# Per-token sums of squares of the differential heads: from columns beside a loaded square to rows at four column positions, and back by way of HBM

## The chip, the cores and the metric

The kernel is one program on one core of a Trainium2 chip. The metric is the device time of one execution in microseconds (us). The chip's engines run side by side and wait for each other by semaphores: TensorE (PE) multiplies matrices (a weight load, LDWEIGHTS, puts the stationary operand into the array, then a MATMUL streams the moving operand past it), VectorE (DVE) and ScalarE (ACT) work on tiles of up to 128 partitions, GpSimd (POOL) does small work and issues some of the transfers (DMAs), and SyncE (SP) issues most transfers. Each engine runs its own instructions in order.

## The reference, cut to what matters

One layer of a decoder: a modulated RMS norm, a joint input projection, two attention branches, gates, an output projection, a gated MLP with a causal convolution, and a last norm. D_MODEL is 1024, SEQ is 512, and all data are float32. The change touches one place, the RMS norm of each differential head's output:

```python
def _diff_attention(q, k, v, lam, lam_init, subln_g, slopes):
    ...
        p = jax.nn.softmax(scores, axis=-1)
        a = p[:, :, 0] - lam * p[:, :, 1]
        return jnp.einsum('bhqs,bshe->bqhe', a.astype(v.dtype), v)
    ...
    out = _rmsnorm(out, subln_g) * (1.0 - lam_init)
```

There are four heads. For each of the 512 tokens of a head, the mean of 128 squares is needed, its inverse root, and a multiplication of the 128 values by that root.

## The kernel before, in words

The program is laid out by hand as a list of matmuls that PE runs in a written order; the other engines' instructions are put in order by a scheduler with priorities. Between about 130 and 235 us PE works on the four differential heads. For each head it makes scores (`sd`), transposes the softmaxed blocks (`td`), multiplies by the values (`od`, a tile with 128 channels as partitions and 512 tokens in a row), and between these it is given other work in steps of three matmuls: projections `pq` and `pk`, gates `pga` and `pgd`, branch products `pA`. Each such step is a tick of `fill`; `after(n, fn)` runs `fn` n ticks later. The tables `STAT_LAG`, `ROW_LAG` and `NORM_LAG` hold, for each head, in how many ticks three things follow the head's `od`.

First, `stats`, STAT_LAG ticks after `od`. ACT has squared `od` into `sq`. Four matmuls with a 128x128 block of `sq` as stationary and one column of ones as moving give `pss`, 128 tokens on partitions and four blocks in columns. DVE takes `pss` over into `ms` (mean of squares plus an epsilon that is scaled by the softmax sums; `rstd_start`). POOL raises it to the power -0.5 and makes one Newton step in four small instructions; the last one writes four columns of the tile `cols`.

Second, `to_rows`, ROW_LAG ticks after `stats`. PE transposes a 128-column window of `cols` (the PE row is called `rs`), ACT copies 32 rows of the result (`rs0p` to `rs3p`), POOL writes four rows to HBM (`rs0d` to `rs3d`) and reads them back broadcast over 128 partitions (`rb`).

Third, `spread`, NORM_LAG ticks after `stats`. DVE multiplies the head's output `of` by `rb`, and ACT and DVE split it into a high and a low part (`vvh`, `vvl`), which the products `pB` use from 237.56 us on.

The tiles `od`, `pss` and `rs` share one PSUM bank (tag "v", one buffer): each must be read out before PE may write the next. The tiles `rs0p` to `rs3p` share one small SBUF buffer (tag "part").

Of the kernel before, what the change touches and what calls it, by code (L numbers as in the profile page):

```python
# [8 lines left out]
F32 = mybir.dt.float32  # L9
F32R = mybir.dt.float32r  # L10
AF = mybir.ActivationFunctionType
ALU = mybir.AluOpType
PSUM = bass.MemoryType.PSUM

P = 128
# [3 lines left out]
NT = S // P  # L19
# [8 lines left out]
HP = 100000  # L28
# [3 lines left out]
G1_AT = 12  # L32
M5_AT = 4
STAT_LAG = (6, 6, 6, 6)
ROW_LAG = (8, 8, 6, 7)
NORM_LAG = (34, 34, 34, 24)
VA_AT = 5
SWA_FILL = (2, 1, 6, 2, 2, 2, 2, 5, 0)
DIFF_FILL = (3, 2, 4, 2)
NCOL = 161  # L40
# [7 lines left out]
def kernel(  # L48
# [19 lines left out]
    nc = tc.nc  # L68
# [3 lines left out]
    def pool(name, bufs=1, space=None, stack=ctx):  # L72
        kw = {} if space is None else {"space": space}
        return stack.enter_context(tc.tile_pool(name=name, bufs=bufs, reuse_waits="tile", **kw))

    cpool = pool("const")
# [3 lines left out]
    dp = pool("rows", space=bass.MemoryType.DRAM)  # L80

    def bank(tag, bufs, shape, name, dt=F32):
        return ps.tile(shape, dt, tag=tag, bufs=bufs, name=name)
# [10 lines left out]
    def vbank(name, shape=(P, S)):  # L94
        return bank("v", 1, list(shape), name)
# [4 lines left out]
    def to_rows(dst, lo, n, name):  # L100
        turned = vbank(name, (P, P))
        nc.tensor.transpose(turned, cols[:, lo + n - P : lo + n], ident)
        part = cpool.tile([32, P], F32, tag="part", name=name + "p")
        with tc.high_priority(offset=2 * HP):
            nc.scalar.copy(part, turned[96:])
        d = dp.tile([n, P], F32, name=name + "d")
        nc.gpsimd.dma_start(d, part[32 - n :])
        nc.gpsimd.dma_start(dst, d.rearrange("k q -> (k q)").partition_broadcast(P))
# [10 lines left out]
    def split(hi, lo, src):  # L119
        return nc.scalar.copy(hi, src), nc.vector.tensor_sub(lo, src, hi.bitcast(F32))  # L120

    def mm3(o, lh, ll, rh, rl, start, stop):
        nc.tensor.matmul(o, lh, rh, start=start, stop=False)  # L123
        nc.tensor.matmul(o, lh, rl, start=False, stop=False)  # L124
        nc.tensor.matmul(o, ll, rh, start=False, stop=stop)  # L125
# [4 lines left out]
    ones = cpool.tile([P, P], F32, name="ones")  # L130
# [5 lines left out]
    mhalf = cpool.tile([P, 4], F32, name="mhalf")  # L136
# [3 lines left out]
    cols = cpool.tile([P, NCOL + 64], F32, name="cols")  # L140
# [8 lines left out]
    root_in = [None]  # L149

    def rstd_start(ssq, n, d, wpool, plus=None):
        ms = wpool.tile([P, n], F32, tag="rs_a", bufs=3, name="ms")
        if plus is None:
            nc.vector.tensor_scalar(ms, ssq, 1.0 / d, EPS, ALU.mult, ALU.add)
        else:
            root_in[0] = nc.vector.scalar_tensor_tensor(ms, ssq, 1.0 / d, plus, ALU.mult, ALU.add)
        r0 = wpool.tile([P, n], F32, tag="rs_c", bufs=3, name="r0")
        nc.gpsimd.tensor_tensor(r0, ms, mhalf[:, :n], ALU.pow)
        return ms, r0
# [92 lines left out]
    ddf = cpool.tile([P, 512], F32, name="ddf")  # L252
    nc.gpsimd.iota(ddf, [[1, 512]], base=-384, channel_multiplier=-1, allow_small_or_imprecise_dtypes=True)
    nc.gpsimd.affine_select(ddf, ddf, [[-1, 512]], ALU.is_ge, NEG, base=384, channel_multiplier=1)
    eps = cpool.tile([P, 1], F32, name="eps")
    nc.gpsimd.memset(eps, EPS)

# [57 lines left out]
    for p in range(KT // 2):  # L315
        for hf in range(2) if p >= 2 else (None,):
            sl = ALL if hf is None else HALVES[hf]
            sq, xx = (a.rearrange("p (a s) -> p a s", a=2)[:, :, sl] for a in (sqs[p], xT[:, p]))
# [15 lines left out]
    r0 = pp.tile([P, NT], F32, tag="rs_c", bufs=3, name="r0")  # L334
    nc.scalar.activation(r0, stat[:, :, 0], AF.Sqrt, bias=eps, scale=1.0 / D)
    ms = pp.tile([P, NT], F32, tag="rs_a", bufs=3, name="ms")
# [59 lines left out]
    for k in range(KT):  # L396
        n = k + 1
# [24 lines left out]
    ap = pool("att", stack=at)  # L422
# [129 lines left out]
    def after(n, fn):  # L552
        later.append([n, fn])
# [175 lines left out]
    emptied, summed = {}, {}  # L729

    def diff_values(h):
        aTh, aTl = aTs[h]
        o = vbank(f"od{h}")
        for k in range(NT):
            q0 = k * P
            mm3(
                o[:, q0:], vv[0][:, h, k * P : (k + 1) * P], vv[1][:, h, k * P : (k + 1) * P],
                aTh[:, k * AW + q0 : k * AW + 512], aTl[:, k * AW + q0 : k * AW + 512],
                k == 0, k == NT - 1,
            )  # L740
        sq = big.tile([P, S], F32, tag="sq2", name=f"sq{h}")
        of = big.tile([P, S], F32, tag=("kvA", "kvB")[h % 2], name=f"of{h}")
        with tc.high_priority(offset=HP):
            nc.scalar.activation(sq, o, AF.Square)
            emptied[h] = nc.scalar.activation(of, o, AF.Copy, scale=sublnc)

        def stats():
            pss = vbank(f"pss{h}", (P, NT))
            for n in range(NT):
                nc.tensor.matmul(pss[:, n : n + 1], sq[:, n * P : (n + 1) * P], ones[:, 0:1], start=True, stop=True)  # L750
            rs = cols[:, NCOL + NT * h : NCOL + NT * h + NT]
            l0, e0 = sums[h][:, 0], sums[h][:, 1]
            nc.gpsimd.tensor_tensor(e0, l0, l0, ALU.mult)
            nc.gpsimd.tensor_scalar_mul(e0, e0, EPS)
            with tc.high_priority(offset=HP):
                ms, r0 = rstd_start(pss, NT, P, ap, plus=e0)
                summed[h] = root_in[0]
                t = ap.tile([P, NT], F32, tag="rs_b", bufs=3, name="rt")
                nc.gpsimd.tensor_tensor(t, r0, r0, ALU.mult)
                nc.gpsimd.tensor_tensor(t, t, ms, ALU.mult)  # L760
                nc.gpsimd.tensor_scalar_add(t, t, -3.0)
                nc.gpsimd.tensor_tensor(rs, t, r0, ALU.mult)
            last = h == DIFF_HEADS - 1
            rb = big.tile([P, S], F32, tag="sq2", name="rb3") if last else ap.tile([P, S], F32, tag="rb", name=f"rb{h}")

            def spread():
                with ExitStack() as place:
                    for b in recent:
                        place.enter_context(tc.issue_after(b.ins))
                    if not last:  # L770
                        place.enter_context(tc.issue_after(summed[h + 1].ins))
                    nc.vector.tensor_mul(of, of, rb)
                with tc.high_priority(offset=HP), ExitStack() as place:
                    if not last:
                        place.enter_context(tc.issue_after(emptied[h + 1].ins))
                    split(vv[0][:, h], vv[1][:, h], of)

            after(ROW_LAG[h], lambda: to_rows(rb, NCOL + NT * h, NT, f"rs{h}"))
            after(NORM_LAG[h], spread)

        after(STAT_LAG[h], stats)


# [114 lines left out]
    for s in range(4 * DIFF_HEADS):  # L898
        h, n = divmod(s, NT)
# [983 lines left out]
```

## Time and profile before

| what | value |
|---|---|
| median of three runs | 676.37 us (676.16 to 676.6) |
| profiled execution, its own time | 676.23 us |
| span of its instructions | 674.4 us |
| PE busy | 664.4 us, 99% of the span |
| DVE, ACT, POOL busy | 564.3, 400.7, 84.9 us |
| granted PE clock, mean | 0.997 |

The profiled execution lies 1.83 us over its span and 0.14 us under the median. In the rows that are shown later, a timeline row reads: start in us, length in us, engine, line of the kernel, operation, output<-inputs, shape, and how many were merged into the row; in brackets stands how long the engine was idle before, and what ended that. A MATMUL's shape names the array's rows and columns in use (128*128) and what streams past. A float32 matmul shows as two records, since it is made in two passes.

### The profile page before, as it was taken

The numbers are of one execution on the slowest core, as the hardware profiler recorded it, in microseconds if no ns is written. First come the engines' busy times: TensorE is split into PE (matmuls) and PEld (weight loads), VectorE is DVE, ScalarE is ACT, GpSimd is POOL, SyncE is SP. The second block draws the span as 40 slices with busy tenths as digits, with TensorE's granted clock in tenths as the row PEclk, the third lists the DMA queues.
The fourth block names the chain that finished last, engine by engine and source line by source line (L and its number), as shares of the span: only waits on it lengthen the run. The fifth ranks groups of instructions, "written<-read, shape, count | busy, mean of one in ns | idle before, by whom it ended". The sixth has DMA issues, their size and how long they took to land.

```text
span 674.4 us, 10800 instructions
## 1 busy us (share of the span) xinstructions
PE 664.4 (99%) x4021; PEld 591.8 (88%) x4021; DVE 564.3 (84%) x1006; ACT 400.7 (59%) x705; POOL 84.9 (13%) x111
## 2 busy tenths in 40 slices
PE   8999999999999999999999999999999999999995
PEld 8888888888888888888899999999999998888884
DVE  6988987778777778954899998888888899979996
ACT  7678787465745423233696655556655666665664
POOL 2000000002212100010010211011111004441200
PEclk9999999999999999999999999999999999999998
DMA  8961232446256798587275988787786559996803
GB/s 352 418 240 62 95 95 63 133 149 182 89 169 193 246 306 267 194 237 241 74 119 140 231 194 200 202 217 162 184 195 178 129 188 208 197 204 185 160 0 125
DMA packets 72212, 121.78 MB, mean 181 GB/s; under 512 B 4256, under 2 KB 48448, under 8 KB 72160
## 3 DMA queue, kind: packets, MB, share of 16 engines
q1 hardware_dynamic: 53248, 95.04, 41.9%
q0 software_dynamic: 18624, 25.84, 22.6%
q8 instruction: 31, 0.51, 0.3%
q10 hardware_dynamic: 288, 0.21, 0.1%
q14 instruction: 21, 0.17, 0.1%
HBM read 118.97 MB, written 2.11 MB: 180 GB/s over the span
## 4 chain that ended last, share of the span: by engine, by line
PE 88%; issue 7%; DVE 2%; DMA 1%; POOL 1%; ACT 0%; SPq 0%; POOLq 0%
PE up L1206 33%; PE dc L1812 7%; PE av L375 3%; PE pga L123 2%; PE pga L125 2%; PE pga L124 2%; PE pgd L123 2%; PE oc L1263 2%; PE pgd L124 2%; PE oc L1266 2%; PE oc L1262 2%; PE pgd L125 2%; PE aqa L372 2%; PE sd L683 2%; PE sw L585 1%
## 5 line engine op out<-in xcount | busy, mean ns | idle before, releaser
L1206 PE MATMUL up<-t,m_whi 128*128 128x256 f32 x512 | 93.2, 283 | 0.0
L1206 PEld LDWEIGHTS up<-t,m_whi 128*128 128x128 f32 x512 | 80.0, 192 | 0.0
L1206 PE MATMUL up<-t,m_wlo 128*128 128x256 f32 x256 | 72.5, 283 | 0.0
L1206 PE MATMUL up<-bh,p_whi 128*128 128x256 f32 x232 | 65.7, 283 | 0.0
L1206 PE MATMUL up<-bl,p_whi 128*128 128x256 f32 x232 | 65.7, 283 | 0.0
L1206 PE MATMUL up<-bh,p_wlo 128*128 128x256 f32 x232 | 65.7, 283 | 0.0
L1206 PEld LDWEIGHTS up<-t,m_wlo 128*128 128x128 f32 x256 | 49.2, 192 | 0.0
L1108 POOL DMA_DIRECT2D s<-in_w_up_dram x21 | 27.0, 1366 | 158.4 <-DMA s<-in_w_up_dram 97.8
L1206 PEld LDWEIGHTS up<-bh,p_wlo 128*128 128x128 f32 x232 | 44.6, 192 | 0.0
L1206 PEld LDWEIGHTS up<-bl,p_whi 128*128 128x128 f32 x232 | 44.6, 192 | 0.0
L1206 PEld LDWEIGHTS up<-bh,p_whi 128*128 128x128 f32 x232 | 44.6, 192 | 0.0
L799 DVE CUSTOM_DVE_ANT_0 ra<-ra,csb 128x1024 f32<-128x1024 f32 x32 | 38.6, 1219 | 4.3 <-DMA ra<-in_w_ada_t_dram 4.3
L1136 ACT CAST m_whi<-s 128x1024 fp32r<-128x1024 f32 x31 | 32.5, 1047 | 15.8 <-DVE s L1130 9.1
L1140 DVE TENSOR_TENSOR m_wlo<-s,m_whi 128x1024 fp32r<-128x1024 f32 x31 | 37.8, 1218 | 1.3 <-ACT m_whi L1136 1.3
L1206 PE MATMUL up<-t,p_whi 128*128 128x256 f32 x176 | 32.2, 284 | 0.0
L1206 PEld LDWEIGHTS up<-t,p_whi 128*128 128x128 f32 x176 | 27.5, 192 | 0.1
L709 ACT ACTIVATE sd<-sd,dmx 128x128 f32<-128x128 f32 (+3 forms) x32 | 17.7, 555 | 14.9 <-DVE dmx L694 14.7
L1136 ACT CAST p_whi<-wa 128x1024 fp32r<-128x1024 f32 x18 | 18.8, 1044 | 12.6 <-DMA s<-in_w_up_dram 7.2
L1213 ACT ACTIVATE gT<-a,cols 128x512 f32<-128x512 f32 x22 | 17.6, 812 | 13.4 <-DVE a L1248 13.0
L1140 DVE TENSOR_TENSOR p_wlo<-wa,p_whi 128x1024 fp32r<-128x1024 f32 x18 | 22.0, 1222 | 4.0 <-ACT p_whi L1136 3.8
L1206 PE MATMUL up<-t,p_wlo 128*128 128x256 f32 x88 | 24.9, 283 | 0.0
L1130 DVE TENSOR_TENSOR s<-s,wa 128x1024 f32<-128x1024 f32 x20 | 24.4, 1220 | 0.1
(551 smaller groups left out, 2037.9 us busy)
## 6 DMA issues: line engine op xcount, KB each, us to landing
ra<-in_w_ada_t_dram SPq DMA_DIRECT2D x32, 512.0 KB, 4.4
wa<-in_w_up_dram SPq DMA_DIRECT2D x22, 512.0 KB, 4.2
s<-in_w_up_dram SPq DMA_DIRECT2D x21, 512.0 KB, 4.6
s<-in_w_up_dram POOLq DMA_DIRECT2D x21, 512.0 KB, 6.9
adaw<-in_w_ada_t_dram SPq DMA_DIRECT2D x15, 512.0 KB, 9.9
a<-in_w_up_dram SPq DMA_DIRECT2D x11, 512.0 KB, 4.7
b<-in_w_down_dram SPq DMA_DIRECT2D x10, 512.0 KB, 4.1
w<-in_w_first_dram SPq DMA_DIRECT2D x8, 512.0 KB, 9.9
```

What stands on the lines that cost most here:

```text
L123: nc.tensor.matmul(o, lh, rh, start=start, stop=False)
L124: nc.tensor.matmul(o, lh, rl, start=False, stop=False)
L125: nc.tensor.matmul(o, ll, rh, start=False, stop=stop)
L375: nc.tensor.matmul(acc[i], ht[:, t : t + P], wts[k][w][:, S:], start=start, stop=stop)
L709: nc.scalar.activation(pm[m], pm[m], AF.Exp, bias=mx[:, m : m + 1], scale=-1.0, accum_out=(l0, l1)[m])
L799: nc.vector.tensor_tensor_reduce(r, r, csb, 1.0, 0.0, ALU.mult, ALU.add, late_mod[:, idx : idx + 1])
L1108: nc.gpsimd.dma_start(dst, upblock(*blk), accum_op=ALU.add)
L1130: nc.vector.tensor_add(src, src, R[J, "a11" if name == "m6" else "a12"])
L1136: nc.scalar.copy(W[J, name][0], R[J, SRC[name]])
L1140: nc.vector.tensor_sub(lo, R[J, SRC[name]], hi.bitcast(F32))
L1206: nc.tensor.matmul(o[u], w[:, k, cu], b[:, k], start=name in ("p1", "m5", "p2") and k == 0 and x == 0, stop=k == 3 and x == 2, skip_group_ ...
L1812: nc.tensor.matmul((bank2[u] if o is None else o)[:, sl], a[:, q, cu], b[:, q, sl], start=first_mm and x == 0, stop=last_mm and x == 2, sk ...
```

## The change: what it does

The constant is now the stationary operand: a 128x32 tile `mean` of 1/128 is loaded, and a 128x128 block of squares streams past it. Each token block goes to another group of 32 columns of the array, so that `pss` holds, at partitions 0, 32, 64 and 96, one row of 128 means for each block (and 31 copies). DVE copies the whole 128x128 to SBUF (`row`, which now shares the "part" buffer). POOL writes the four rows to HBM (`back`) and reads them back with tokens on partitions (`ms`, 128x4 single words). Then POOL adds the epsilon, which DVE's `ms` did in its scalar_tensor_tensor before, and goes on as before. `to_rows` follows 9 to 10 ticks later than before, and `spread` 2 ticks later.

```diff
--- before.py
+++ after.py
@@ -32,8 +32,8 @@
 G1_AT = 12
 M5_AT = 4
 STAT_LAG = (6, 6, 6, 6)
-ROW_LAG = (8, 8, 6, 7)
-NORM_LAG = (34, 34, 34, 24)
+ROW_LAG = (17, 17, 16, 17)
+NORM_LAG = (36, 36, 36, 26)
 VA_AT = 5
 SWA_FILL = (2, 1, 6, 2, 2, 2, 2, 5, 0)
 DIFF_FILL = (3, 2, 4, 2)
@@ -252,6 +252,8 @@
     ddf = cpool.tile([P, 512], F32, name="ddf")
     nc.gpsimd.iota(ddf, [[1, 512]], base=-384, channel_multiplier=-1, allow_small_or_imprecise_dtypes=True)
     nc.gpsimd.affine_select(ddf, ddf, [[-1, 512]], ALU.is_ge, NEG, base=384, channel_multiplier=1)
+    mean = cpool.tile([P, 32], F32, name="mean")
+    nc.gpsimd.memset(mean, 1.0 / P)
     eps = cpool.tile([P, 1], F32, name="eps")
     nc.gpsimd.memset(eps, EPS)
 
@@ -745,21 +747,28 @@
             emptied[h] = nc.scalar.activation(of, o, AF.Copy, scale=sublnc)
 
         def stats():
-            pss = vbank(f"pss{h}", (P, NT))
+            pss = vbank(f"pss{h}", (P, P))
             for n in range(NT):
-                nc.tensor.matmul(pss[:, n : n + 1], sq[:, n * P : (n + 1) * P], ones[:, 0:1], start=True, stop=True)
-            rs = cols[:, NCOL + NT * h : NCOL + NT * h + NT]
+                nc.tensor.matmul(pss[32 * n : 32 * n + 32], mean, sq[:, n * P : (n + 1) * P], start=True, stop=True)
+            row = cpool.tile([P, P], F32, tag="part", name=f"row{h}")
+            with tc.high_priority(offset=HP):
+                summed[h] = nc.vector.tensor_copy(row, pss)
             l0, e0 = sums[h][:, 0], sums[h][:, 1]
             nc.gpsimd.tensor_tensor(e0, l0, l0, ALU.mult)
             nc.gpsimd.tensor_scalar_mul(e0, e0, EPS)
-            with tc.high_priority(offset=HP):
-                ms, r0 = rstd_start(pss, NT, P, ap, plus=e0)
-                summed[h] = root_in[0]
-                t = ap.tile([P, NT], F32, tag="rs_b", bufs=3, name="rt")
-                nc.gpsimd.tensor_tensor(t, r0, r0, ALU.mult)
-                nc.gpsimd.tensor_tensor(t, t, ms, ALU.mult)
-                nc.gpsimd.tensor_scalar_add(t, t, -3.0)
-                nc.gpsimd.tensor_tensor(rs, t, r0, ALU.mult)
+            back = dp.tile([NT, P], F32, name=f"back{h}")
+            nc.gpsimd.dma_start(back, row[0:P:32])
+            ms = ap.tile([P, NT], F32, tag="rs_a", bufs=3, name=f"ms{h}")
+            nc.gpsimd.dma_start(ms, back.rearrange("n q -> q n"))
+            rs = cols[:, NCOL + NT * h : NCOL + NT * h + NT]
+            nc.gpsimd.tensor_tensor(ms, ms, e0, ALU.add)
+            r0 = ap.tile([P, NT], F32, tag="rs_c", bufs=3, name="r0")
+            nc.gpsimd.tensor_tensor(r0, ms, mhalf, ALU.pow)
+            t = ap.tile([P, NT], F32, tag="rs_b", bufs=3, name="rt")
+            nc.gpsimd.tensor_tensor(t, r0, r0, ALU.mult)
+            nc.gpsimd.tensor_tensor(t, t, ms, ALU.mult)
+            nc.gpsimd.tensor_scalar_add(t, t, -3.0)
+            nc.gpsimd.tensor_tensor(rs, t, r0, ALU.mult)
             last = h == DIFF_HEADS - 1
             rb = big.tile([P, S], F32, tag="sq2", name="rb3") if last else ap.tile([P, S], F32, tag="rb", name=f"rb{h}")
```

How the instructions move on PE, shown for the third head (h = 2). Before, the transposition `rs` stood behind a `pA` step and ahead of the transpositions `td`:

```order
L123 MATMUL pA_2137<-outah,wba_h 128x512
L124 MATMUL pA_2137<-outal,wba_h 128x512
L125 MATMUL pA_2137<-outah,wba_l 128x512
L102 MATMUL rs_2147<-ident,cols 128x128 [waits DVE_49,Pool_49]
L724 MATMUL td_2_2154<-ident,sd_2_0_2066 128x128 x3
L123 MATMUL pA_2137<-outah,wba_h 128x512
```

That place holds only the `pA` and `td` rows now. Just ahead of the fourth head's `od` there were only gates before:

```order
L123 MATMUL pga_2201<-hThA,wga_h 128x512
L124 MATMUL pga_2201<-hTlA,wga_h 128x512
L125 MATMUL pga_2201<-hThA,wga_l 128x512
L123 MATMUL od_2214<-aTh_2018,vvh 128x512 [waits Activation_49]
L124 MATMUL od_2214<-aTl_2019,vvh 128x512 [waits DVE_49]
```

There the transposition stands now, and PE goes from it straight to `od`, which writes the same bank:

```order
L123 MATMUL pga_2211<-hThA,wga_h 128x512
L124 MATMUL pga_2211<-hTlA,wga_h 128x512
L125 MATMUL pga_2211<-hThA,wga_l 128x512
L102 MATMUL rs_2224<-ident,cols 128x128 [waits Pool_49]
L123 MATMUL od_2231<-aTh_2030,vvh 128x512 [waits Activation_49]
L124 MATMUL od_2231<-aTl_2031,vvh 128x512 [waits DVE_49]
L125 MATMUL od_2231<-aTh_2030,vvl 128x512
```

So `rs` moved past six steps of three matmuls and seven `td` matmuls, to the last row before `od`. ACT's copy `rs2p`, which empties the bank, moved with it: it now lies between `rs` and `od`.

On POOL, between the chains of the second and the third head (`dls` are the softmax sums, of which the epsilon is made). Before, from the power of the second head to its two DMAs:

```order
L158 TENSOR_TENSOR r_1847<-ms,mhalf 128x4 [waits DVE_49]
L759 TENSOR_TENSOR rt<-r_1847 128x4 [waits Pool_49]
L760 TENSOR_TENSOR rt<-rt,ms 128x4 [waits Pool_49]
L761 TENSOR_SCALAR rt<-rt 128x4 [waits Pool_49]
L762 TENSOR_TENSOR cols<-rt,r_1847 128x4 [waits Pool_49]
L107 DMA rs1d<-rs1p 4x128 [waits Activation_49]
L753 TENSOR_TENSOR dls_1727<-dls_1727 128x4 [waits DVE_49]
L754 TENSOR_SCALAR dls_1727<-dls_1727 128x4 [waits Pool_49]
```

With the change, for the same head:

```order
L760 DMA back_1854<-row_1850 4x128 [waits DVE_49]
L762 DMA ms_1856<-back_1854 128x4x1 [waits DMASW4_49]
L764 TENSOR_TENSOR ms_1856<-ms_1856,dls_1469 128x4 [waits DMASW5_49,Pool_49]
L766 TENSOR_TENSOR r_1859<-ms_1856,mhalf 128x4 [waits Pool_49]
L768 TENSOR_TENSOR rt<-r_1859 128x4 [waits Pool_49]
L769 TENSOR_TENSOR rt<-rt,ms_1856 128x4 [waits Pool_49]
L770 TENSOR_SCALAR rt<-rt 128x4 [waits Pool_49]
L771 TENSOR_TENSOR cols<-rt,r_1859 128x4 [waits Pool_49]
L757 TENSOR_TENSOR dls_1727<-dls_1727 128x4 [waits DVE_49,Activation_49]
L758 TENSOR_SCALAR dls_1727<-dls_1727 128x4 [waits Pool_49]
L107 DMA rs1d<-rs1p 4x128 [waits Activation_49]
```

Two DMAs and an addition now stand ahead of the power, and each of them waits for the landing of the one before.

On DVE, the third head. Before, the `ms` instruction stood ahead of a reduction over `ra` (a row of the adaLN weights):

```order
L714 SCALAR_TENSOR_TENSOR sd_2_0_2066<-sd_2_1_2068,dls_1963,sd_2_0_2066 128x384 [waits DVE_49]
L156 SCALAR_TENSOR_TENSOR ms<-pss_2083,dls_1727 128x4 [waits PE_49,Pool_49]
L799 ISA ra_2110,late_mod<-ra_2110,csb 128x1024 [waits DMAHW2_49]
L799 ISA late_mod 128x1
L431 TENSOR_TENSOR aTl_2019<-td_1_2100,aTh_2018 128x2x128 [waits Activation_49]
```

With the change, its successor, the copy of `pss`, stands behind that reduction:

```order
L716 SCALAR_TENSOR_TENSOR sd_2_0_2078<-sd_2_1_2080,dls_1968,sd_2_0_2078 128x384 [waits DVE_49]
L808 ISA ra_2127,late_mod<-ra_2127,csb 128x1024 [waits DMAHW2_49]
L808 ISA late_mod 128x1
L755 COPY row_2100<-pss_2095 128x128 [waits DMASW6_49,DMASW4_49,PE_49]
L433 TENSOR_TENSOR aTl_2031<-td_1_2117,aTh_2030 128x2x128 [waits Activation_49]
L781 TENSOR_TENSOR of_1806<-of_1806,rb_1866 128x512 [waits DMASW7_49]
```

The copy moved behind one long instruction, and it waits for two landings besides, those of the last users of the shared "part" buffer.

## The prediction

> **What bounds the kernel now.** I read the page first, then PE's waits, then the timeline of the stage around the change.
>
> ```profile
> span 674.4 us, 10800 instructions
> PE 664.4 (99%) x4021; PEld 591.8 (88%) x4021; DVE 564.3 (84%) x1006; ACT 400.7 (59%) x705; POOL 84.9 (13%) x111
> PE ava L241 <- POOL ones L131: 1.1, 1, 1.1
> PE av L375 <- ACT hThA L361: 0.6, 1, 0.6
> PE aka L267 <- DVE cols L271: 0.5, 1, 0.5
> ```
>
> The first two lines are the page's, the other three are all waits of PE in the whole run: 2.2 us. PE bounds the kernel everywhere, and it has no idle time later that could take up a delay. A nanosecond saved on PE shortens the run, and one that PE waits lengthens it by as much. The other engines matter only where PE waits for them. So two questions decide: what the sums cost PE, and whether `cols` is ready when PE reaches the moved transposition `rs`.
>
> Places of PE's timeline: the four `pss` groups, what follows the first, and the rows ahead of which `rs` now stands (found by the order of instructions).
>
> ```profile
> 149.14 0.95 PE L750 MATMUL pss<-ones,sq 128*128 128x1 f32 x8
> 149.95 0.42 PE L724 MATMUL td<-ident,sd 128*128 128x128 f32 x2
> 164.67 0.39 PE L123 MATMUL pk<-hThA,w_h 128*128 128x512 f32 x1
> 174.28 0.50 PE L750 MATMUL pss<-ones,sq 128*128 128x1 f32 x4
> 188.43 0.39 PE L123 MATMUL pga<-hThA,wga_h 128*128 128x512 f32 x1
> 198.72 0.50 PE L750 MATMUL pss<-ones,sq 128*128 128x1 f32 x4
> 209.89 0.39 PE L123 MATMUL od<-aTh,vvh 128*128 128x512 f32 x1
> 215.92 0.61 PE L750 MATMUL pss<-ones,sq 128*128 128x1 f32 x5
> 228.56 0.39 PE L123 MATMUL pgd<-hThA,wgd_h 128*128 128x512 f32 x1
> 237.56 0.39 PE L123 MATMUL pB<-vvh,wbd 128*128 128x512 f32 x1
> ```
>
> From sums to transposition PE thus has 15.53, 14.15, 11.17 and 12.64 us of other work in the four heads. That is the cover of the new round trip.
>
> **The sums on PE.** A group takes 149.95 - 149.14 = 0.81 us now: eight passes, each held up by its own 128-column load. Nothing in the trace runs on four column positions, but the sliding-window values run on two (128*64):
>
> ```profile
> 88.72 0.39 PE L125 MATMUL pk<-hThB,w_l 128*128 128x512 f32 x1
> 89.03 3.25 PE L636 MATMUL oa<-pT,va 128*64 128x256 f32 x32
> 92.21 0.44 PE L585 MATMUL sw<-ka,qa 128*128 128x128 f32 x2
> 10.70 1.73 PE L301 MATMUL av<-cs,adaw 128*128 128x128 f32 x14
> ```
>
> The last row prices a pass of 128 columns with the array undivided: less about 0.27 us of tail, 1.46 us for 13 steps, 0.112 us. By the program's shapes the `oa` group is 24 passes of 256 and 8 of 128 columns, 24 x 0.224 + 8 x 0.112 = 6.3 us one after another. It took 92.21 - 89.03 = 3.2 us, so two positions run at once, with 0.1 us at the entry and hardly more at the exit. The new group is eight passes of 128 columns: 0.22 us if four positions run at once, 0.45 us if two, 0.90 us if none, and 0.1 to 0.3 us for going in and out. I take 0.5 us, between four and two. Gain: 4 x 0.3 = 1.2 us. Ends: four at once with cheap switching, 0.4 us a group, gain 1.6 us; none at once, 1.1 us, a loss of 1.2 us.
>
> **DVE.** The copy of 128x128 replaces a small instruction.
>
> ```profile
> 150.20 0.16 DVE L156 SCALAR_TENSOR_TENSOR ms<-pss,dls 128x4 f32<-128x4 f32 x1
> 176.96 0.16 DVE L156 SCALAR_TENSOR_TENSOR ms<-pss,dls 128x4 f32<-128x4 f32 x1
> 191.10 0.29 DVE L431 TENSOR_TENSOR aTl<-td,aTh 128x128 fp32r<-128x128 f32 x1
> 200.03 1.22 DVE L799 CUSTOM_DVE_ANT_0 ra<-ra,csb 128x1024 f32<-128x1024 f32 x1
> 216.98 0.16 DVE L156 SCALAR_TENSOR_TENSOR ms<-pss,dls 128x4 f32<-128x4 f32 x1
> ```
>
> I price the copy at 0.29 us, as DVE's reading of another 128x128 of PSUM; the 0.13 us more on DVE lies beside PE's work. In the third head it now stands behind the `ra` instruction and starts at about 201.2. The copies end at about 150.5, 177.3, 201.5 and 217.3. What PE still has ahead of `rs` is then 164.67 - 150.5 = 14.2, 188.43 - 0.3 - 177.3 = 10.8, 209.89 - 0.3 - 201.5 = 8.1 and 228.56 - 217.3 = 11.3 us (in the middle two DVE sets the start, and PE comes 0.3 us sooner; in the others both shift). The wait for the "part" buffer costs nothing: the DMAs of the head before have landed over 5 us earlier; without that cover each would cost what is left of its landing.
>
> **POOL and the round trip.** These rows price the two new DMAs and the root:
>
> ```profile
> 157.88 0.78 POOL L107 DMA_DIRECT2D rs0d<-rs0p  x1 [4.03 <-ACT rs0p L105]
> 162.68 0.65 POOL L108 DMA_DIRECT2D rb<-rs0d  x1 [2.74 <-DMA rs0d<-rs0p]
> 177.21 1.05 POOL L158 TENSOR_TENSOR r<-ms,mhalf 128x4 f32<-128x4 f32 x1 [13.89 <-DVE ms L156]
> 180.60 0.60 POOL L762 TENSOR_TENSOR cols<-rt,r 128x4 f32<-128x4 f32 x1
> 183.09 0.62 POOL L107 DMA_DIRECT2D rs1d<-rs1p  x1 [1.89 <-ACT rs1p L105]
> 186.81 0.63 POOL L108 DMA_DIRECT2D rb<-rs1d  x1 [2.22 <-DMA rs1d<-rs1p]
> 217.23 1.04 POOL L158 TENSOR_TENSOR r<-ms,mhalf 128x4 f32<-128x4 f32 x1 [4.89 <-DVE ms L156]
> 219.77 0.20 POOL L762 TENSOR_TENSOR cols<-rt,r 128x4 f32<-128x4 f32 x1
> L1108 POOL DMA_DIRECT2D s<-in_w_up_dram x21: 1274/1283/2407, 336.0 to 520.4; - x21
> rb<-rs2d POOLq DMA_DIRECT2D x1, 256.0 KB, 7.1
> ```
>
> - Hand-over from DVE to POOL: `r` follows `ms` by 0.1 us (216.98 + 0.16 to 217.23); a DMA follows ACT's copy (ending 157.57, shown below) by 0.3 us. I take 0.2 us.
> - `back`, 4x128 words to HBM, is the same transfer as `rs0d`. From its issue to POOL's next issue 162.68 - 157.88 = 4.80 us, and 186.81 - 183.09 = 3.72 us, the longest and the shortest of four. I take the middle, 4.26 us.
> - `ms`, 512 single words, is not in the trace. Lower end: the 3.72 us of a write of as many bytes. Upper end: 7.5 us, the longest `rb` (7.1 us to landing) and a wake-up of 0.4. It is nearest to the small write, with a longer issue, since `s` with its 512 rows takes 1.28 us to issue and `rs1d` 0.62: 4.26 + 0.7 = 5.0 us.
> - The addition: 0.3 us (between 0.2 us, like POOL's short instruction at 219.77, and 1.0 us, like its first after a wait).
> - The root and its step, from the start of `r` to the end of `cols`: 3.99 us (177.21 to 181.20) and 2.74 us (217.23 to 219.97) are the ends of four; middle 3.4 us.
>
> Sum from the end of the copy: 0.2 + 4.26 + 5.0 + 0.3 + 3.4 = 13.2 us. All low: 0.2 + 3.72 + 3.72 + 0.2 + 2.74 = 10.6 us. All high: 0.3 + 4.80 + 7.5 + 1.0 + 3.99 = 17.6 us.
>
> Against the cover of 14.2, 10.8, 8.1 and 11.3 us, PE waits 0, 2.4, 5.1 and 1.9 us. I take 0.5 us off the third, since a pause in the second head lets DVE's queue ahead of the third copy catch up: 4.6 us. All low, only the third head waits, 2.5 us. All high, PE waits 3.4 + 6.8 + 9.5 + 6.3 = 26 us.
>
> **The bank.** In the third head `od` stands right behind `rs` in the same PSUM bank, so PE must wait for ACT's copy too:
>
> ```profile
> 157.00 0.27 PE L102 MATMUL rs<-ident,cols 128*128 128x128 f32 x1
> 157.31 0.26 ACT L105 COPY rs0p<-rs 32x128 f32<-32x128 f32 x1
> ```
>
> From the start of `rs` to the end of the copy 0.57 us, and a hand-over: 0.6 us, at least 0.5 even where `cols` is early. In the other heads `od` or the next user of the bank comes 2.8 us or more later, and the copy is hidden by the steps between.
>
> **Later.** POOL's longer chain holds ACT's first softmax of the head after next, which reuses the sums tile. The addition ends about 10 us after the copy, 160.3 in the first head and 187 in the second; ACT falls behind while PE waits anyway. The last `rb` lands later: `rs` at 228.6 + 1.9, the ACT copy 0.6, the write 4.3, `rb` about 4.5, hence 239.9, then DVE and ACT 2.0 us for `vvh` and `vvl`. PE's `pB` begins at 237.56 + 1.9 and needs the fourth head nine matmuls of 0.23 us later, 241.5. So it is just covered; a landing of 7.1 us would cost 2.6 us more. I count 0.
>
> Sum: -1.2 + 2.4 + 4.6 + 1.9 + 0.6 = +8.3 us against the profiled execution's 676.23 us, which is 0.14 us under the median: 684.5 us.
>
> **Rivals.**
>
> The round trip fits. If each DMA trip took 2.2 us to POOL's next instruction, the chain would be 0.2 + 2.2 + 2.2 + 0.3 + 3.4 = 8.3 us; only the third head would wait, 0.2 + 0.6 us, and the time would be 676.23 - 1.2 + 0.8 = 675.8 us, not slower. It decides from a trip of 2.4 us on, where the third head's wait and the bank eat the gain (0.2 + 4.8 + 0.3 + 3.4 - 8.1 + 0.6 = 1.2 us). Against it: the shortest of four trips took 3.72 us. I give it a tenth. The Trainium skill's page "DMA: Bandwidth & Descriptors" (section "Anatomy of one DMA") fits about 2.0 us plus bytes over bandwidth for a transfer on this path, which would give this rival's time. This trace's trips are 1.7 to 2.8 us longer.
>
> The clock falls. PE's granted clock fell after the last matmul, and at the start the first matmuls were slow:
>
> ```profile
> 666.35 0.28 PE L1812 MATMUL dc<-p4wh,p4a 128*128 128x256 f32 x1
> 670.40:674.40 4.00, 0.00 (x0) 0.00 (x0) 0.00 (x0) 0.00 (x0) 0.28 (x1) 0.50 0.37 133
> 1.12 4.25 PE L241 MATMUL ava<-ones 128*128 128x128 f32 x20 [1.12 <-POOL ones L131]
> ```
>
> The last matmul ended at 666.6, and by 670.4 the clock was 0.50 (the number after POOL's). The first 20 passes took 4.25 us in place of 20 x 0.112 = 2.2 us. So an idle PE loses its clock within 3.8 us, and a start from cold costs 2 us. The third head's two waits, 4.6 + 0.6 us, are longer than that by 1.4 us, which is less than the uncertainty of the sum, so I take somewhat under half. One such fall gives 686.5 us. The page "TensorE: Matmul & The Clock Gate" of the Trainium skill (Part 1) has the rule behind it: a whole idle window of about 3.4 us halves the clock, and windows run freely; by that a wait of 5.2 us would hold a whole window about half the time, as the rows leave it too.
>
> The column positions don't run at once: a loss of 1.2 us in place of the gain, 676.23 + 9.5 + 1.2 = 686.9 us. The `oa` rows speak against it.
>
> **How the numbers follow.** What a measurement here can tell from no change is about 0.2%, 1.35 us. Waits as summed, clock kept: 0.55. With a fall of the clock: 0.24. Positions one after another: 0.07. Round trip fits: 0.10, which is within 0.2%. A gain over 0.2% needs no wait at all and sums at their cheapest (1.6 us): 0.04. That makes slower 0.86, same 0.10, faster 0.04. Range: the low end has all trips low, 676.23 - 1.2 + 2.5 + 0.6 = 678.1, and I put 677.0, half-way to the fit; the high end has the middle sum, a fall of the clock and the `pB` wait of 2.6 us, 689. The all-high sum is left out, since four heads would have to be high at once.
>
> **What would show it.** Right: `pss` groups of about 0.5 us on PE; PE waiting for POOL's `cols` at `rs` in the heads two to four, longest in the third, and for ACT at `od` there; trips of 3.7 to 5 us for `back` and `ms`. Wrong: trips near 2 us, a copy of `pss` much earlier than 201 us in the third head, or waits of PE under 1 us. Then the time is the old one less the gain of the sums.

## Result and the profile after

The changed kernel takes 686.46 us, median of five runs (684.62 to 688.05), against 676.37 us before: a ratio of 1.0147, 95% interval 1.0133 to 1.0161. It is slower by 10.1 us, 2.0 us more than the 684.5 us forecast. The profiled execution spans 684.5 us, 10.1 us more than the one before, and the last matmul starts 9.7 us later than before; the other 0.4 us lie behind the last matmul.

The head of the page of the kernel after:

```profile
span 684.5 us, 10819 instructions
PE 668.0 (98%) x4021; PEld 591.0 (86%) x4021; DVE 564.8 (83%) x1006; ACT 400.4 (59%) x705; POOL 93.5 (14%) x124
```

All waits of PE in it (microseconds in total, times, longest):

```profile
PE rs L102 <- POOL cols L771: 4.0, 2, 3.2
PE ava L241 <- POOL ones L131: 1.1, 1, 1.1
PE pB L123 <- ACT vvh L120: 1.0, 1, 1.0
PE av L377 <- ACT hThA L363: 0.7, 1, 0.7
PE pB L124 <- DVE vvl L120: 0.6, 1, 0.6
PE aka L269 <- DVE cols L273: 0.4, 1, 0.4
PE od L123 <- ACT rs2p L105: 0.4, 1, 0.4
```

Four of these lines were not there before: `rs` waiting for `cols` (two of the four heads), `pB` waiting for the fourth head's values (two lines), and `od` waiting for the bank. Together 6.0 us. PE's busy time rose too, by 3.6 us, although the sums became shorter; most of that is a clock at half speed, shown below.

**The sums.** The first group on PE's timeline, with the matmul ahead of it and the first behind:

```profile
149.47 0.39 PE L125 MATMUL pga<-hThA,wga_l 128*128 128x512 f32 x1
149.78 0.43 PE L752 MATMUL pss<-sq,mean 128*32 128x128 f32 x8
150.14 0.44 PE L726 MATMUL td<-ident,sd 128*128 128x128 f32 x2
```

From the matmul ahead of the group to the first behind it took 0.67 us; before it was 1.03 us. In the four heads the work behind the sums moved up by 0.32 to 0.35 us, 1.33 us in all. The trace's single records show why: the four positions' passes start within 20 ns of one another, and the second four follow 0.13 us later.

**The third head's round trip.** POOL's timeline:

```profile
200.79 0.60 POOL L760 DMA_DIRECT2D back<-row  x1 [8.37 <-DVE row L755]
204.13 0.81 POOL L762 DMA_DIRECT2D ms<-back  x1 [2.74 <-DMA back<-row]
...
206.88 0.20 POOL L764 TENSOR_TENSOR ms<-ms,dls 128x4 f32<-128x4 f32 x1 [0.37 <-DMA ms<-back]
207.17 2.09 POOL L766 TENSOR_TENSOR r<-ms,mhalf 128x4 f32<-128x4 f32 x1
209.34 0.81 POOL L768 TENSOR_TENSOR rt<-r 128x4 f32<-128x4 f32 x1
210.22 1.06 POOL L769 TENSOR_TENSOR rt<-rt,ms 128x4 f32<-128x4 f32 x1
211.36 1.09 POOL L770 TENSOR_SCALAR rt<-rt 128x4 f32<-128x4 f32 x1
212.54 0.20 POOL L771 TENSOR_TENSOR cols<-rt,r 128x4 f32<-128x4 f32 x1
```

From its issue to the next on POOL `back` took 3.34 us, `ms` 2.75 us to the addition, and the root and its step 5.57 us (207.17 to 212.74). PE's timeline at that place:

```profile
209.16 0.39 PE L125 MATMUL pga<-hThA,wga_l 128*128 128x512 f32 x1
212.80 0.33 PE L102 MATMUL rs<-ident,cols 128*128 128x128 f32 x1 [3.25 <-POOL cols L771]
213.52 0.57 PE L123 MATMUL od<-aTh,vvh 128*128 128x512 f32 x1 [0.39 <-ACT rs2p L105]
213.88 0.63 PE L124 MATMUL od<-aTl,vvh 128*128 128x512 f32 x1
```

PE had nothing else to do from 209.55 to 212.80, then 0.39 us more for the bank. And behind it a 512-column matmul takes 0.63 us in place of 0.39, and the next starts 0.43 us later in place of 0.23.

**The clock.** The same stretches of time as windows (length, busy time of PE, PEld, DVE, ACT and POOL with counts, then PE's granted clock, DMA share and GB/s):

```profile
207.00:210.40 3.40, 2.55 (x12) 1.74 (x10) 3.40 (x5) 0.69 (x2) 3.16 (x4) 1.00 0.76 243
210.40:213.80 3.40, 0.61 (x2) 0.42 (x3) 1.97 (x4) 0.26 (x1) 2.21 (x4) 1.00 0.71 245
213.80:217.20 3.40, 3.40 (x13) 3.13 (x13) 0.00 (x0) 0.03 (x1) 0.59 (x1) 0.50 0.82 283
217.20:220.60 3.40, 3.40 (x16) 2.77 (x16) 0.00 (x0) 1.91 (x3) 0.58 (x1) 1.00 0.28 60
244.50:247.90 3.40, 1.83 (x8) 0.99 (x7) 2.62 (x4) 1.85 (x4) 0.53 (x1) 1.00 0.16 58
247.90:251.40 3.50, 3.50 (x9) 2.73 (x10) 3.50 (x6) 1.53 (x2) 0.50 (x1) 0.51 0.82 249
```

The clock is 1.00 while PE waits and 0.50 for the 3.41 us behind, twice: after the third head's wait (213.81 to 217.22 us in the trace's record of the clock), and after the wait at `pB` (247.94 to 251.35). Each time PE does 1.65 to 1.7 us less work.

**The fourth head's values.** The chain from its `rs` to `pB`, on the timeline of all engines:

```profile
234.31 0.33 PE L102 MATMUL rs<-ident,cols 128*128 128x128 f32 x1 [0.78 <-POOL cols L771]
...
235.26 0.61 POOL L107 DMA_DIRECT2D rs3d<-rs3p  x1 [1.01 <-ACT rs3p L105]
...
239.28 0.59 POOL L108 DMA_DIRECT2D rb<-rs3d  x1 [3.40 <-DMA rs3d<-rs3p]
...
245.28 0.69 DVE L781 TENSOR_TENSOR of<-of,rb 128x512 f32<-128x512 f32 x1 [5.80 <-DMA rb<-rs3d]
246.00 0.62 ACT L120 CAST vvh<-of 128x512 fp32r<-128x512 f32 x1 [6.30 <-DVE of L781]
...
246.67 0.49 PE L123 MATMUL pB<-vvh,wbd 128*128 128x512 f32 x1 [0.97 <-ACT vvh L120]
...
247.76 0.66 PE L124 MATMUL pB<-vvl,wbd 128*128 128x512 f32 x1 [0.59 <-DVE vvl L120]
```

From `rs` to `of` 10.97 us, of which the transfer `rb` takes 6.00. PE is at `pB` 0.97 us too early for `vvh`, and 0.59 us for `vvl`.

**The sum, from the same matmuls paired in both traces:** sums -1.33, third head's `rs` and `od` +4.11, clock +1.65, fourth head's `rs` +1.01, `pB` +2.02, clock +1.7, and +0.56 from the first microseconds of the program: +9.7 us. The last term is probably spread between executions and no effect of the change: the kernel lag_last below, whose program up to there is that of before, lost 0.33 us there (its wait of `aka` for `cols` is 1.0 us in place of 0.5).

### The profile page after: what moved, and what is told of

Same layout as the page of the kernel before. It is cut to its first block, busy times and chain, and to the rows that moved or that the text cites. A ratio compares the mean times of both kernels' runs of the same rounds, so it can differ in the third digit from the quotient of the medians.

```text
span 684.5 us, 10819 instructions
## 1 busy us (share of the span) xinstructions
PE 668.0 (98%) x4021; PEld 591.0 (86%) x4021; DVE 564.8 (83%) x1006; ACT 400.4 (59%) x705; POOL 93.5 (14%) x124
## 4 chain that ended last, share of the span: by engine, by line
PE 80%; issue 9%; DMA 6%; DVE 3%; ACT 1%; POOL 0%; POOLq 0%; ACTq 0%; DVEq 0%
PE up L1215 32%; PE dc L1821 9%; PE av L377 3%; PE oc L1275 2%; PE oc L1272 2%; PE oc L1271 2%; PE pgd L123 2%; PE pgd L124 2%; PE pgd L125 2%; PE aqa L374 2%; DMA ms<-back 1%; DMA back<-row 1%; PE sw L587 1%; DMA w<-in_w_first_dram 1%; PE pq L125 1%
```

## Experiments

All ratios are to the kernel before, run beside it on the same chip (676.3 to 676.6 us median there); the base of each edit is named. The diffs show the lines that matter; `...` stands for lines that are not shown.

**1. The lags without the trip.** From the kernel before, only the tables of lags, which set how late `rs` and the products stand: in all heads (lags_alone), in the first three (lags_early), in the fourth (lag_last).

```diff
-ROW_LAG = (8, 8, 6, 7)            # before
-NORM_LAG = (34, 34, 34, 24)
+ROW_LAG = (17, 17, 16, 17)        # lags_alone
+NORM_LAG = (36, 36, 36, 26)
+ROW_LAG = (17, 17, 16, 7)         # lags_early
+NORM_LAG = (36, 36, 36, 24)
+ROW_LAG = (8, 8, 6, 17)           # lag_last
+NORM_LAG = (34, 34, 34, 26)
```

Expected of lags_alone:

> The old sums and no trip through HBM, but the table of lags of the changed kernel, so the transpositions rs stand where the change put them. Theory (the loss is PE waiting for cols, and later for vv, because the trip is longer than its cover): cols is ready long before each rs, so only the bank is left, a wait of od for ACT's copy of about 0.4 to 0.6 us in the third head, and up to 0.6 us at the fourth head of the first pB, whose values are made later; 676.4 + 0.5 to 1.2 = 676.9 to 677.6 us, no fall of the clock. Rival (the place of rs and of the products behind it costs most of the loss by itself): 680 us or more.

Expected of lags_early:

> The kernel before with the changed kernel's lags in the first three heads alone; the fourth head as before. Theory now: only the wait of od for ACT's copy in the third head, 0.4 us, with 0.2 to 0.3 us of pipeline: 676.5 + 0.6 = 677.1 us. Rival (the shifted order of the first three heads costs what the lags cost together): 679 us or more.

Expected of lag_last:

> The kernel before with the changed kernel's lags in the fourth head alone (ROW_LAG 7 to 17, NORM_LAG 24 to 26): no trip, old sums, the first three heads as before. Theory now (the later place of rs in the fourth head makes that head's values late for the first pB, whatever made cols late): PE waits 0.9 to 1.2 us for vvh and 0.6 for vvl at pB, 676.5 + 2.1 = 678.6 us, and 1.6 us more in executions where the clock falls behind it. Rival (the cost of the lags alone came from the first three heads, the bank or a shifted order): within 0.2% of the kernel before, 676.5 us.

Measured: lags_alone 679.45 us (1.0040, 1.0027 to 1.0053), lags_early 677.12 us (1.0009, 1.0000 to 1.0018), lag_last 679.53 us (1.0045, 1.0031 to 1.0058). PE's waits that are new in the profile of each, first lags_alone:

```profile
PE pB L123 <- ACT vvh L120: 1.1, 1, 1.1
PE pB L124 <- DVE vvl L120: 0.6, 1, 0.6
PE od L123 <- ACT rs2p L105: 0.4, 1, 0.4
```

lag_last:

```profile
PE pB L123 <- ACT vvh L120: 1.4, 1, 1.4
PE pB L124 <- DVE vvl L120: 0.6, 1, 0.6
```

lags_early has the line of `od` alone. So the wait at `pB` is no effect of the trip: it comes from the lag of the fourth head, with the old sums and no transfer added. I had given the lags 0.5 to 1.2 us; they cost 2.9 us, and lag_last alone 3.2. The bank in the third head costs 0.6 to 0.8 us, as expected.

The five executions of lags_alone also price a fall of the clock in one and the same program: the profiled one took 680.88 us with a mean granted clock of 0.993 and a fall behind `pB` in its trace; the other four took 679.20 to 679.47 us at 0.996 to 0.998, which is the clock of the kernel before (0.996 to 0.998). That is 1.4 to 1.7 us. Of the five of lag_last two show a mean clock of 0.993 and 0.994. The five of the changed kernel spread over 3.4 us in the same manner, with mean clocks of 0.988 to 0.994.

**2. The sums without a wait for the trip.** From the changed kernel: the root takes a constant in place of the sums of squares (they are left out of the result), and `back` and a read of it that nobody uses are issued behind the root. trip_unwaited has the changed kernel's lags, sums_alone the old lags, sums_dry the old lags and no transfers.

```diff
-nc.gpsimd.dma_start(back, row[0:P:32])
-nc.gpsimd.dma_start(ms, back.rearrange("n q -> q n"))
+nc.gpsimd.tensor_scalar_add(ms, e0, 1.0)
...
+nc.gpsimd.dma_start(back, row[0:P:32])                      # not in sums_dry
+nc.gpsimd.dma_start(unread, back.rearrange("n q -> q n"))   # not in sums_dry
```

Expected of trip_unwaited:

> The changed kernel, with its sums at four column positions, its copy to a row and both transfers, but the root takes a constant in place of the sums that come back, and the transfers are issued behind the root: nothing waits for them. Theory: all waits for cols go; the sums give 1.3 us, the bank takes 0.4 to 0.6 us, the fourth head's values as much as in the lags alone: 675.5 to 676.3 us, clock 1.0 throughout. Rival (the new sums, their copy on DVE or the added DMA traffic cost the time): 680 us or more, and the time of the changed kernel nearly unaltered.

Expected of sums_alone:

> The sums at four column positions, the copy to a row and both transfers, with nothing waiting for the transfers (the root takes a constant in place of the sums), and all lags as in the kernel before. Theory now (what the trip_unwaited kernel lost came with the lags, not with the sums, the copy or the transfers): 676.4 - 1.3 = 675.1 us, no wait of PE beyond those of the kernel before, no fall of the clock. Rival (the transfers' traffic makes the fourth head's values late by itself): a wait for vvh at pB and 677 us or more.

Expected of sums_dry:

> As the kernel of the sums alone (old lags, the root takes a constant in place of the sums), but without the two transfers: the sums at four column positions and the copy to a row are all that is left of the change. Theory (the small transfers hold up the weight loads, whose cast on ACT starts 0.6 us later in the third head, so that DVE is late and PE waits for sd and aTl): those two waits go and the gain of the sums is seen whole, 676.4 - 1.4 = 675.0 us. Rival (PE, now faster, runs into a weight load that comes when it comes, transfers or not): the waits stay and the time is 676.2 to 676.8 us.

Measured: trip_unwaited 682.07 us (1.0082, 1.0067 to 1.0097), sums_alone 676.74 us (1.0002, 0.9992 to 1.0012), sums_dry 676.90 us (1.0007, 0.9998 to 1.0016). My expectations missed all three times.

In trip_unwaited the wait for `cols` is gone, as expected, but the values of the fourth head are later still:

```profile
PE pB L123 <- ACT vvh L120: 2.7, 1, 2.7
PE pB L124 <- DVE vvl L120: 0.6, 1, 0.6
```

Its `rs` stood at 228.48 us and ACT copied it only at 230.38, since a cast of weights ahead of the copy in ACT's queue waited for its load until 229.30. So with the lags of the change 5.5 us are lost without any wait for the trip.

With the old lags no wait at `pB` is left, so the sums and the transfers alone don't make the fourth head late, and by experiment 1 the lag alone does. How late still depends on what lies around it: 1.1 us at `vvh` in lags_alone and 2.7 in trip_unwaited; why that load came late there stays open. But the gain of the sums isn't seen either. Each group is shorter by 0.36 us in both traces, 1.4 us in all, and 1.0 (sums_alone) and 1.4 us (sums_dry) are lost again in the third head. All lines of sums_dry there:

```profile
PE td L726 <- DVE sd L716: 0.8, 1, 0.8
PE od L124 <- DVE aTl L433: 0.2, 1, 0.2
```

DVE is late because ACT's cast of `wga` is late (194.94 us; 194.21 before), which waits for its load. The load and POOL's transfer `rb` of the head before are under way together: `rb` was issued at 188.20 us in sums_dry and at 186.81 before, since the root with a constant has no sums to wait for and stands ahead of `rb` on POOL; the load took 5.7 us to land in place of 4.5. Where `rs` stands later `rb` does too, behind the load's issue, and the load landed in 3.3 us (experiment 5a, the load issued at 189.51 and `rb` at 191.27). The theory that the small transfers hold up the load fell, for sums_dry has none. That `rb`'s place does it fits all three traces, but it was not tried by itself.

**3. PE busy in its waits.** From the changed kernel, with spare matmuls whose product nobody reads: 14 ahead of `rs` in the third head, 4 in the fourth, 9 ahead of the fourth head in the first `pB`.

```diff
     def to_rows(dst, lo, n, name):
+        busy = {"rs2": 14, "rs3": 4}.get(name, 0)
+        if busy:
+            spare = vbank(name + "w")
+            for _ in range(busy):
+                nc.tensor.matmul(spare, hTh[0][:, :P], hTh[1], start=True, stop=True)
         turned = vbank(name, (P, P))
...
+                    if n == 2:
+                        for _ in range(9):
+                            nc.tensor.matmul(spare, hTh[0][:, :P], hTh[1], start=True, stop=True)
```

Expected:

> The changed kernel with spare matmuls of 512 columns (0.23 us each) in the places where PE waited: 14 ahead of rs in the third head, 4 ahead of it in the fourth, 9 ahead of the fourth head of the first pB. PE waits no less than before, but is not idle. Theory (part of the loss, about 1.65 us each, is two falls of the clock that idle time brings about): no fall in the records, and 686.5 - 3.3 = 683.2 us, within 0.6 us either way, since the spare matmuls (3.2, 0.9 and 2.1 us) are about as long as the waits (3.25, 0.78 and 1.56 us). Rival (the falls come by themselves or cost nothing that waiting would not): 686 us or more.

Measured: 685.65 us (1.0141, 1.0125 to 1.0157). In the profiled execution the clock stays at 1.00 (mean 0.998); one of the other three took 688.22 us at a mean of 0.995. The third head's wait as a window, with PE busy and the clock at 1.00:

```profile
209.20:212.70 3.50, 3.41 (x16) 2.48 (x14) 3.05 (x5) 0.00 (x0) 3.09 (x5) 1.00 0.82 256
```

A wait of PE in the same kernel:

```profile
PE pB L128 <- ACT vvh L125: 1.0, 1, 1.0
```

It is as long as in the changed kernel, behind the 9 spare matmuls, and the one for `vvl` is too (0.59 us).

In the third head `od` starts 4.16 us later than before the change, as in the changed kernel (4.11), and the 1.65 us of half clock that followed there are gone. So there idle time, not the stage, brings the fall about. At `pB` the 1.7 us are gone too, but this shows less: PE was idle there as long as in the changed kernel. What differs is where the idle time lies. The falls come at the edges of windows of 3.41 us (last section), and here an edge at 247.04 us (counted back in steps of 3.413 us from the fall at 680.53 us, behind the last matmul) divides it:

```profile
243.62:247.04 3.42, 2.69 (x12) 1.88 (x11) 1.14 (x2) 0.41 (x1) 0.13 (x1) 1.00 0.98 379
247.04:250.45 3.41, 2.56 (x10) 1.91 (x11) 2.91 (x4) 1.74 (x3) 0.42 (x1) 1.00 0.72 223
```

PE was busy for 2.6 to 2.7 us in each, against 1.83 us in the changed kernel's window ahead of its second fall. The total moved by 0.8 us only, and the two intervals overlap: the fourth head's values came 2 us later (12.97 us from `rs` to `of` in place of 10.97; the row's write took 5.1 us to land in place of 3.5, `rb` 6.4 in place of 6.0), so the 9 spare matmuls were added to the wait instead of standing in for it. I had not expected that, and the time of 683.2 us is missed for this reason.

**4. The trip with the old sums.** From the kernel before, with the changed lags: the columns go out as 512 single words and come back as such.

```diff
-ms, r0 = rstd_start(pss, NT, P, ap, plus=e0)
...
+near = ap.tile([P, NT], F32, tag="near", bufs=2, name=f"near{h}")
+summed[h] = nc.vector.scalar_tensor_tensor(near, pss, 1.0 / P, e0, ALU.mult, ALU.add)
...
+nc.gpsimd.dma_start(back.rearrange("n q -> q n"), near)
...
+nc.gpsimd.dma_start(ms, back.rearrange("n q -> q n"))
```

Expected:

> The kernel before with the changed kernel's lags and a trip of the sums through HBM (columns out and in as 512 single words each way, by POOL's queue), but with the old sums: one 128-column pass each with a load of its own, columns at once. Theory (waits for the trip and lateness of the fourth head's values make the loss, the sums at four positions give 1.3 us of it back): 686.5 + 1.3 = 687.8 us, between 686 and 690, with PE waiting for cols at rs in the third head for 3 us or more. Rival (the sums at four positions, or the row copy on DVE, carry part of the loss): 685 us or less.

Measured: 719.59 us (1.0620, 1.0597 to 1.0642). PE's wait for `cols`:

```profile
PE rs L102 <- POOL cols L769: 34.7, 4, 10.0
```

The two transfers (KB each, median us from issue to landing):

```profile
back<-near POOLq DMA_DIRECT2D x4, 2.0 KB, 10.3
ms<-back POOLq DMA_DIRECT2D x4, 2.0 KB, 6.5
```

This is no clean undoing of the sums, as I had meant it: the write of single words takes 10.3 us in place of 3.0, and the read 6.5 in place of 3.1. As a trip made 10 us longer it serves: PE then waits in all four heads. So the 3.0 us of the changed kernel go with the sums lying in rows, which are written as four pieces of 128 words. Why the read, of the same form in both, takes twice as long here stays open.

**5. Other ways for the sums.** (a) columns_by_pe, from the changed kernel: PE turns the row back, DVE adds `e0` from PSUM, nothing goes by way of HBM; ROW_LAG (14, 14, 13, 13).

```diff
-nc.gpsimd.dma_start(back, row[0:P:32])
-nc.gpsimd.dma_start(ms, back.rearrange("n q -> q n"))
-nc.gpsimd.tensor_tensor(ms, ms, e0, ALU.add)
...
+nc.tensor.transpose(back, row, ident)        # 4 or 5 steps behind the sums
...
+nc.vector.tensor_add(ms, back[:, 0:P:32], e0)
```

Expected:

> The sums of the changed kernel, but PE itself turns the row back into columns: a transposition of 128x128 some 4 or 5 steps behind the sums, then DVE's addition from PSUM and the same root; nothing goes by way of HBM. Theory (sums gain 0.33 us a group, the trip loses): four transpositions of 0.11 us each are added, rs stands early enough not to wait; 676.4 - 1.3 + 0.45 = 675.5 us, and up to 0.6 us more for the fourth head's values, no wait for cols on PE, clock 1.0. It would be the fastest of all so far. Rival (four column positions or the copy to a row cost something that the profile hides): 677 us or more.

Measured: 676.12 us, 11 runs (0.9992, 0.9984 to 1.0001): not told apart from the kernel before. By pairs of matmuls the sums give 1.41 us and the four transpositions take 0.5 back, 0.88 us between the first head and the fourth; PE's waits are the three at the program's start and no others. The waits of the changed kernel are all gone, with the same sums.

(b) root_in_rows, from the kernel before and with its lags: nothing is turned at all; `e0` is added by four more passes at the four positions, and POOL takes the root on the row, 128x128.

```diff
-ms, r0 = rstd_start(pss, NT, P, ap, plus=e0)
...
+nc.tensor.matmul(pss[32 * n : 32 * n + 32], wide[:, 32 * n : 32 * n + 32], ident, start=False, stop=True)
...
+nc.gpsimd.tensor_tensor(r0, row, mhalf[:, 0:1].to_broadcast([P, P]), ALU.pow)
```

Expected:

> A version in which nothing is turned: the sums at four column positions, four more passes there that add the eps term (columns spread over 32 by POOL, the identity moving), DVE's copy to a row, the root and its step by POOL on the row (128x128 instead of 128x4), and the row goes to HBM and comes back spread out as before. The four transpositions rs and the trip of the sums are gone; the lags are those of the kernel before. Theory (PE bounds): four groups 0.33 us shorter, four transpositions of 0.11 us gone, four groups of passes of about 0.2 us added: 676.5 - 1.3 - 0.45 + 0.8 = 675.5 us, no wait of PE beyond those of the kernel before. Rival (POOL's five instructions on 128x128, of which no run so far has a row, take over 10 us and make the values late): 678 us or more.

Measured: 710.51 us (1.0499, 1.0485 to 1.0513). The rival held, through one instruction on POOL's timeline:

```profile
183.12 20.77 POOL L767 TENSOR_TENSOR r<-row,mhalf 128x128 f32<-128x128 f32 x1 [1.27 <-DVE row L765]
203.97 1.52 POOL L768 TENSOR_TENSOR row<-row,r 128x128 f32<-128x128 f32 x1
```

The power takes 20.8 us on 128 columns and 1.05 us on 4, an estimate of 0.16 us for each column more; POOL is then too late for the next head's `wide`, and PE waits 18.9 us for it, and 5.9 us more at `pB`.

**6. The fourth head's `rs` early, with the trip.** From the changed kernel:

```diff
-ROW_LAG = (17, 17, 16, 17)
-NORM_LAG = (36, 36, 36, 26)
+ROW_LAG = (17, 17, 16, 7)
+NORM_LAG = (36, 36, 36, 24)
```

Expected:

> The changed kernel with the fourth head's lags put back (ROW_LAG 17 to 7, NORM_LAG 26 to 24), so that rs of this head stands about 10 us of PE's work earlier. Theory now (from the sums to the values of the fourth head is one chain, and cols come when they come): PE waits for cols there about 10.5 us instead of 0.8, and not at all for vvh and vvl at pB (2.0 us less); one fall moves from pB to rs. 686.5 + 9.9 - 2.0 = 694.4 us, between 692 and 696. Rival (the lag of the fourth head by itself makes the lateness at pB, as in the kernel without a trip, and an early rs cures it): 684.5 us or less.

Measured: 689.27 us (1.0173, 1.0149 to 1.0197). Both numbers missed. `rs` moved by 6.8 us of PE's work and not by 10, as I had misread the order. The two waits of `rs` came to 8.5 us, and `pB` waits for nothing:

```profile
PE rs L102 <- POOL cols L771: 8.5, 2, 5.1
```

So with the trip an early `rs` cures the lateness at `pB`, and PE pays 5.1 us in its own queue for that; against the changed kernel 5.4 us more at `rs` and 2.7 of half clock ahead of `pB` beyond what the changed kernel has, less 1.1 at the old place of `rs`, 2.0 at `pB` and 1.7 of half clock there: 3.3 us more to the last matmul. Neither place is free: the chain from the sums to the values is longer than the work that PE has between them.

## Why the prediction was right, and where not

The mechanism was right as far as `rs`: the sums get cheaper by about a microsecond, and PE, which has no slack, waits for `cols` where `rs` now stands. The rival of a trip that fits is out, since it needs 2.2 us to POOL's next instruction; measured were 3.24 to 3.34 us for `back` in the three heads that matter (2.09 in the first) and up to 3.58 for `ms`. The rival of positions one after another is out (0.36 us gained a group). Term by term:

- Sums on PE: -1.2 forecast, -1.33 measured. Four positions at once, with little at entry and exit.
- The round trip was priced too high: `back` 2.1 to 3.3 us (forecast 4.26), `ms` 2.75 to 3.6 (5.0). The reason is the choice of the middle of the old trips, and of a dearer `ms` for its 512 words. The Trainium skill's page "DMA: Bandwidth & Descriptors" (section "Anatomy of one DMA") gives about 2.0 us for such a transfer; the landings here (3.0 and 3.1 us in the median) lie between that and my price.
- The root was priced too low where it mattered: 3.4 us forecast, 5.57 in the third head, 4.5 in the fourth, 3.03 in the second. The two errors cancel in part: the chain from the end of the copy was 12.2 us in the third head and 11.9 in the fourth (13.2 forecast), 10.4 in the second and 9.6 in the first, both under the 10.6 that I had as the lowest.
- Waits of PE for `cols`: second head 0 (forecast 2.4: `cols` ended at 187.88 us and PE came at 188.24), third 3.25 (4.6), fourth 0.78 (1.9). In the third head the row's copy also ended at 200.50 in place of 201.5.
- The bank: 0.39 us of wait behind a transposition of 0.33; 0.6 to 0.8 us by experiment 1 (forecast 0.6).
- `pB`: counted as nothing, with "just covered"; it is 2.0 us. This is the step that failed. The later place of `rs` in the fourth head makes its values late even without a trip (experiment 1). My own sum already had them at 241.9 us where PE needs them at 241.5, and I priced `rb` at 4.5 us, its landing in this head before; in the six traces with this head's `rs` at the changed lag it took 5.0 to 6.4 us. The 2.6 us that I gave as the price of a longer landing was the nearer value.
- The clock: two falls, 3.35 us, where I gave one a chance of 0.24. Experiment 3 shows that the first goes with PE's idle time; the second fell away there with the wait still as long, across a window's edge. I weighed the idle time against a whole window, and gave no chance to a fall at `pB`.

Sum: the waits came to 7.1 us in place of 9.5, and the clock to 3.35 in place of 0. Without the falls the change would have cost 5.8 us (8.3 forecast), so the time came out close to the forecast by luck: the waits were 2.4 us less, and falls that the forecast had only beside it, as a rival, gave 3.35 us more.

## To carry to other kernels

Where one engine has no slack, follow a moved step to the end of its chain, to the last consumer, and give every transfer on the way its longest landing in the trace: here 3.7 of 9.7 us lay not at the moved transposition but 12 us behind it, at the first product that reads the head's values. A lag that covers a longer trip takes its cover from the chain behind it, so try the new lags with the old work first; that one run would have shown 2.9 of the 10.1 us. And price a wait of PE with the clock behind it: here 1.65 to 1.7 us on top of waits of 1.6 to 3.6 us, in some executions and not in others where the wait is short.

## What the runs showed of the hardware

- PE's clock can halve for 3.41 us after a stretch that isn't wholly idle. The two falls of the changed kernel lie on one grid (starts at 213.81 and 247.94 us, ten times 3.413 apart), and every fall between the first and the last matmul in these traces lasts one to four times 3.41 us. Ahead of the second, PE was busy for 1.83 of 3.40 us. The Trainium skill's page "TensorE: Matmul & The Clock Gate" (Part 1) asks for a whole idle window of about 3.4 us; the length of the window agrees, the need for a whole one doesn't. A wait of 0.78 us (fourth head) brought no fall, and the wait at `pB` of 1.7 us did so in one of five executions of lags_alone by their mean clocks, so where the window's edge falls seems to matter; experiment 3, with the idle time at `pB` divided by an edge and no fall, agrees. The share of busy time alone doesn't settle it: in experiment 6 a window with 1.69 us busy (226.10 to 229.51) brought no fall. The least idle share was not measured.
- POOL's short instructions can take as long as the DVE instruction beside them. A window over the root of the changed kernel's third head (the third number after the length is DVE's busy time), and behind it one over the root of the fourth head in experiment 6:

```profile
207.10:212.80 5.70, 2.45 (x12) 1.69 (x10) 5.27 (x8) 0.59 (x2) 5.25 (x5) 1.00 0.78 255
```

The same in the kernel of experiment 6:

```profile
230.60:232.90 2.30, 0.01 (x1) 0.01 (x2) 0.00 (x0) 0.00 (x0) 1.87 (x5) 1.00 0.00 0
```

  The same five instructions on 128x4 take 5.6 us beside a busy DVE and 2.2 us beside an idle one. In the third head the last three long ones end at 210.15, 211.28 and 212.45 us, each 0.14 to 0.16 us behind the moment at which one DVE instruction of 128x1024 gave way to what follows it (210.00, 211.14 and 212.29). The Trainium skill's page "GPSIMD Engine Reference" (section "Specifications") has the two engines share their SBUF interfaces, with contention where DVE reads two inputs from SBUF; these rows agree, though no run was made for it. The three DVE instructions here read two tiles of SBUF. In the second head DVE was busy too, but mostly with instructions that read the scores or `pA` out of PSUM; there the addition, the power and the three instructions behind it took 2.2 us together:

```profile
184.50:186.85 2.35, 2.35 (x14) 2.00 (x13) 1.84 (x10) 2.05 (x8) 1.89 (x5) 1.00 0.62 214
```

  The next one, `cols`, took 1.00 us, beside a DVE instruction of 128x1024 that reads two tiles of SBUF.
- A write of 512 single words to HBM took 10.3 us to land, one of the same words as four rows 3.0 us.
